# One instruction order in place of another: the Tile scheduler of a two-layer trunk set to its timeline simulation

## Chip, cores and metric

The kernel runs on one core of a Trainium2 chip. The metric is the device time of one execution in microseconds (us), as the median of several runs. An execution under the profiler gives the trace; its times are counted from the start of its span. TensorE (PE) is the matrix engine, PEld its weight loads, VectorE is DVE, ScalarE is ACT, GpSimd is POOL, SyncE is SP (SPq its DMA queue).

## What is computed

Two layers over 528 tokens (16 learned ones ahead of 512) of 1024 channels, in float32. Cut to what matters, each layer of the reference is:

```python
xn = _rmsnorm(h, pre_norm_g[l])
proj = xn @ w_in[l] + b_in[l]
c_h, c_b, c_c, c_z, r_q, r_k, r_v, r_z, g_a, g_b = jnp.split(proj, split_at, axis=-1)
y_a = _short_conv_branch(c_h, c_b, c_c, c_z, conv_w[l], conv_b[l], w_conv_out[l])
y_b = _retention_branch(r_q, r_k, r_v, r_z, ret_gn_g[l], w_ret_out[l])
y = jax.nn.sigmoid(g_a) * y_a + jax.nn.sigmoid(g_b) * y_b
y = y @ w_o[l]
h = h + _rmsnorm(y, post_norm_g[l])
```

The retention branch has four heads. Each takes scores of rotated queries and keys times a decay, multiplies them with the values, and normalizes the result per token and head: `(out - mu) * rsqrt(var + eps)`, times a weight and a silu gate.

## The kernel before

Channels lie on the 128 partitions, tokens along the free dimension, cut into two halves of 264. A float32 product is made of three matmul passes: every operand is split (`split`, L141) into a high half, a cast on ScalarE (L142), and a low half, the difference on VectorE (L143); TensorE then adds high x high, high x low and low x high in PSUM. Weights come from HBM through SyncE's queue into a ring of buffers `raw`; their halves are `whi` and `wlo` (`whd` and `wld` for a fourth combination). The activations' halves are `Xh` and `Xl`.

The large projections are made by `Group` (L284): a block scheme with seven products instead of eight, so weights are first added on VectorE (L307 `raw`, L314 `raw`, L315 `t`), and partial results in the PSUM banks `pa`, `pb`, `pc` are evicted by ScalarE (`put`, L325) and added on VectorE (L356). Matmuls of these groups are L279. `Std` (L660, matmuls L648 by `ktiles`) makes plain tiles, at the start, at the layer boundary and for the first heads of the second layer. `RetOut` makes the output projection of a head (matmuls L244).

A retention head ends in a norm that crosses four engines. `attend` (L481) leaves outputs in PSUM; ScalarE squares them (L492), VectorE scales them by the weight (L493) and adds the squares (L496). `rstd_token` then sums over the partitions with small matmuls against `ones_d` (L370), VectorE adds the epsilon (L374, `nv`), GpSimd takes the power -1/2 (L375, `ny`), and `spread` brings the result back to all partitions by matmuls with the identity (L384), copied by ScalarE (L387). `normed` multiplies with it (L514).

```python
pp = pslot()
for c in range(nch):
    nc.tensor.matmul(pp[0:sc, 0, c:c + 1], sums[:, t0 + c * sc:t0 + (c + 1) * sc], ones_d[:, 0:1],
                     start=True, stop=True)
...
with tc.high_priority():
    nc.vector.tensor_scalar(v, pp[0:sc, 0, 0:nch], scale, eps, op0=ALU.mult, op1=ALU.add)
nc.gpsimd.tensor_tensor(y, v, mhalf[0:sc, 0:nch], op=ALU.pow)
```

The same two functions serve the layer boundary. `wo_half` makes the output projection of one token half; `norms` (L742) normalizes it, adds the residual, sums squares (L641: `ysum` for the projection, `hsum` for the residual), and scales for the next layer:

```python
def scaled(k):
    nc.vector.scalar_tensor_tensor(YB[:, k, sl], hts[k][:, sl], gpre_sb[:, l + 1, k:k + 1], R[:, sl],
                                   op0=ALU.mult, op1=ALU.mult)
    split(*plain(half, k), YB[:, k, sl])
```

So for each of eight channel blocks one L761 is followed by a high half (ScalarE, L142) and a low half (VectorE, L143, `Xl` for the first token half, `r` or `Xl` for the second). `opening` then runs the first tiles of the second layer block by block (L648).

The order of each engine's instructions is not the order of the source. `tile.TileContext` (L1256) collects the program with its dependencies and runs a simulation of the engines: whenever an engine is free there, it takes, of the instructions that are ready at that simulated time, the one with the highest priority. Priority is program order, raised inside `tc.high_priority()`. The order found so is fixed in the program; on the chip every engine works through its own list in order, and waits on semaphores.

## Time and profile before

| what | value |
|---|---|
| median of 3 runs | 1605.07 us (1603.92 to 1609.26) |
| the profiled execution | 1600.25 us, span 1598.4 us, mean granted clock 0.995 |
| TensorE busy | 1553.9 us (97%), 11762 instructions |
| weight loads busy | 1494.1 us (93%) |
| VectorE busy | 1168.9 us (73%), 1702 instructions |
| ScalarE busy | 910.2 us (57%), 1763 instructions |
| GpSimd busy | 28.9 us (2%), 23 instructions |
| HBM | 168.21 MB read, 4.26 MB written, 108 GB/s over the span |

How to read it: the busy time of an engine counts the time in which one of its instructions ran. A matmul's time overlaps that of the next one, so what one costs is read from how many start in a stretch, not from its own length. The granted clock is a share of full speed. In a timeline the first number is the start, the second the length, and the brackets hold the idle time of the engine before the instruction with what ended it. A power on GpSimd is one instruction, L375.

### The profile page before, as it was taken

How to read it: one execution, taken by the hardware profiler on the slowest of the kernel's cores; microseconds unless marked ns; L12 is line 12 of the kernel's file. 1: busy time of each engine (PE TensorE's matmuls, PEld its weight loads, DVE VectorE, ACT ScalarE, POOL GpSimd, SP SyncE). 2: the span in 40 equal slices, each digit the busy share in tenths (PEclk: the TensorE clock that was granted, in tenths of full speed). 3: DMA queues.
4: the chain of work that ended last, by engine and by line, in shares of the span. 5: the costliest groups of instructions: out<-in, count | busy, mean ns of one | idle time of the engine just before them, and what ended most of it. 6: DMA issues, size and time to landing. Idle time of an engine off the chain costs nothing.

```text
span 1598.4 us, 29227 instructions
## 1 busy us (share of the span) xinstructions
PE 1553.9 (97%) x11762; PEld 1494.1 (93%) x11762; DVE 1168.9 (73%) x1702; ACT 910.2 (57%) x1763; POOL 28.9 (2%) x23
## 2 busy tenths in 40 slices
PE   9999999899999999999999999999999999999998
PEld 9989999898999999999999998998998999999986
DVE  6996966776776788866376889678777777997542
ACT  6675565464565466655345666655654655676531
POOL 0000000001000000000000000000000000000000
PEclk9999999999999999999999999999999999999999
DMA  7132332232222243335321223222322223334421
GB/s 263 67 113 73 106 107 89 83 108 97 89 103 87 91 141 128 133 123 180 119 101 53 100 94 113 103 103 95 111 93 80 101 98 119 132 126 145 142 98 53
DMA packets 86039, 174.37 MB, mean 109 GB/s; under 512 B 11280, under 2 KB 15888, under 8 KB 85904
## 3 DMA queue, kind: packets, MB, share of 16 engines
q1 hardware_dynamic: 85760, 172.50, 31.2%
q8 instruction: 92, 1.51, 0.4%
q14 instruction: 43, 0.35, 0.1%
q10 hardware_dynamic: 144, 0.01, 0.0%
HBM read 168.21 MB, written 4.26 MB: 108 GB/s over the span
## 4 chain that ended last, share of the span: by engine, by line
PE 79%; DVE 10%; ACT 5%; issue 3%; DMA 3%; POOL 1%; SPq 0%; DVEq 0%; POOLq 0%; ACTq 0%
PE pb L279 25%; PE pp L244 15%; PE pc L279 13%; PE pp L648 7%; PE pa L279 6%; PE pp L481 4%; PE pp L1122 3%; PE pb L648 3%; DVE wlo L143 2%; PE pp L422 2%; DMA raw<-in_w_in 2%; ACT whi L142 2%; DVE r L143 1%; PE pp L384 1%; PE pp L447 1%
## 5 line engine op out<-in xcount | busy, mean ns | idle before, releaser
L143 DVE TENSOR_TENSOR wlo<-raw,whi 128x1024 fp32r<-128x1024 f32 (+2 forms) x358 | 392.7, 1107 | 120.4 <-ACT whi L142 117.5
L142 ACT CAST whi<-raw 128x1024 fp32r<-128x1024 f32 (+2 forms) x358 | 339.4, 959 | 227.8 <-PE pp L244 63.7
L279 PE MATMUL pb<-Xh,whi 128*128 128x264 f32 (+2 forms) x1008 | 287.7, 285 | 2.2 <-ACT pa L335 1.2
L279 PE MATMUL pb<-Xl,whi 128*128 128x264 f32 (+2 forms) x1008 | 285.0, 283 | 0.0
L279 PE MATMUL pb<-Xh,wlo 128*128 128x264 f32 (+2 forms) x1008 | 284.7, 283 | 0.1
L244 PE MATMUL pp<-r,whi 128*128 128x264 f32 (+1 forms) x1152 | 251.2, 325 | 5.6 <-ACT r L142 4.8
L279 PE MATMUL pc<-Xh,whi 128*128 128x264 f32 (+2 forms) x672 | 194.4, 289 | 8.1 <-ACT f L325 7.8
L244 PEld LDWEIGHTS pp<-r,whi 128*128 128x128 f32 x1152 | 176.3, 188 | 23.7 <-ACT r L142 5.9
L279 PEld LDWEIGHTS pb<-Xh,whi 128*128 128x128 f32 x1008 | 189.6, 188 | 4.4 <-ACT pa L335 1.6
L279 PE MATMUL pc<-Xl,whi 128*128 128x264 f32 (+2 forms) x672 | 192.0, 286 | 0.0
L279 PE MATMUL pc<-Xh,wlo 128*128 128x264 f32 (+2 forms) x672 | 191.5, 285 | 0.0
L279 PEld LDWEIGHTS pb<-Xl,whi 128*128 128x128 f32 x1008 | 189.6, 188 | 0.6
L279 PEld LDWEIGHTS pb<-Xh,wlo 128*128 128x128 f32 x1008 | 189.3, 188 | 0.5 <-DVE wlo L143 0.3
L244 PE MATMUL pp<-r,wlo 128*128 128x264 f32 (+1 forms) x576 | 153.1, 321 | 1.4 <-DVE wlo L143 1.4
L307 DVE TENSOR_TENSOR raw<-raw 128x512 f32<-128x512 f32 x168 | 115.1, 686 | 41.4 <-DMA raw<-in_w_in 40.9
L279 PEld LDWEIGHTS pc<-Xh,whi 128*128 128x128 f32 x672 | 128.0, 190 | 12.3 <-ACT f L325 11.2
L279 PEld LDWEIGHTS pc<-Xl,whi 128*128 128x128 f32 x672 | 127.9, 190 | 0.4
L279 PEld LDWEIGHTS pc<-Xh,wlo 128*128 128x128 f32 x672 | 127.8, 190 | 0.3
L244 PEld LDWEIGHTS pp<-r,wlo 128*128 128x128 f32 x576 | 95.3, 188 | 9.8 <-DVE wlo L143 2.0
L279 PE MATMUL pb<-Xh,whd 128*128 128x264 f32 (+2 forms) x336 | 96.7, 288 | 1.1 <-ACT f L325 1.1
L279 PE MATMUL pa<-Xh,whi 128*128 128x264 f32 (+2 forms) x336 | 96.7, 288 | 0.0
L279 PE MATMUL pa<-Xl,whi 128*128 128x264 f32 (+2 forms) x336 | 95.7, 285 | 0.0
(219 smaller groups left out, 3300.3 us busy)
## 6 DMA issues: line engine op xcount, KB each, us to landing
raw<-in_w_in SPq DMA_DIRECT2D x426, 256.0 KB, 2.9
raw<-in_w_ro SPq DMA_DIRECT2D x32, 512.0 KB, 3.2
raw<-in_w_in SPq DMA_DIRECT2D x20, 512.0 KB, 4.8
raw<-in_w_co SPq DMA_DIRECT2D x16, 512.0 KB, 3.2
raw<-in_w_o SPq DMA_DIRECT2D x16, 512.0 KB, 3.9
Dsb<-in_decay SPq DMA_DIRECT2D x8, 520.0 KB, 3.9
h1d<-f SPq DMA_DIRECT2D x8, 264.0 KB, 4.5
f<-h1d SPq DMA_DIRECT2D x8, 264.0 KB, 4.3
```

The lines of the kernel that those rows point to most:

```text
L142: nc.scalar.copy(dst_hi, src)
L143: nc.vector.tensor_tensor(dst_lo, src, dst_hi.bitcast(F32), op=ALU.subtract)
L244: nc.tensor.matmul(banks[i][:, 0:cols.n], wt(k)[:, msl], xs(k)[:, sl], start=(k == 0 and a == 0), stop=(k == nk - 1 and a == 2),)
L279: nc.tensor.matmul(o[:, 0:n], wt[:, k, :], xs[:, blk, k, HALF - n:], start=(first and k == 0 and a == 0), stop=(k == 3 and a == 2), skip_g ...
L307: nc.vector.tensor_tensor(r[:, 512:], r[:, 512:], r[:, 0:512], op=ALU.add)
L384: nc.tensor.matmul(pp[:, c // per, (c % per) * sc:(c % per + 1) * sc], y[:, c:c + 1].to_broadcast([sc, P]), ident[0:sc, 0:sc], start=True, ...
L422: nc.tensor.matmul(pp[0:kn, n + i, 0:cols.n], k[dt][x][:, k0:k0 + kn] if j < 4 else k8[:, dt * 2 + x, :], q[dt][y][:, sl], start=(dt == 0 ...
L447: nc.tensor.transpose(pp[0:kn, b, v * P:(v + 1) * P], vt[v][:, k0:k0 + kn] if j < 4 else v8[:, v, :], ident)
L481: nc.tensor.matmul(pp[:, b, lo_ - banks[b][0]:hi_ - banks[b][0]], V[j][x][0:kn, v * P:(v + 1) * P], S[0:kn, SOFF[j] + lo_ - q0:SOFF[j] + h ...
L648: nc.tensor.matmul(o, wt(k), xs[:, i0:], start=(k == 0 and a == 0), stop=(k == KD - 1 and a == 2))
L1122: nc.tensor.matmul(o, x[:, xs], wo[k][half][w], start=(k == 0 and a == 0), stop=(k == KD - 1 and a == 2))
```

## The change

The `TileContext` gets one more argument. The simulation that orders the instructions is then the framework's timeline simulation and no longer its core simulation. Instructions, tiles and dependencies are the same; only the order on each engine differs, and with it which buffer a tile gets and which wait stands where.

```diff
-    with tile.TileContext(nc) as tc:
+    with tile.TileContext(nc, schedule_with_timeline_sim=True) as tc:
         trunk(tc, *args)
```

GpSimd's order is the same in both. On SyncE some loads change places, mostly the decay tables and the inputs at the boundary. Three places of the other engines follow; names are the program's, with the number of the tile behind the underscore.

**First place: TensorE at the norm of the first head.** The groups beside it are those of the convolution, `pb_1726`, `pa_108` and `pc_1727`. Before:

```order
L279 MATMUL pb_1726<-Xh,whi_1565 128x264
L279 MATMUL pb_1726<-Xl,whi_1565 128x264
L279 MATMUL pb_1726<-Xh,wlo_1566 128x264
L370 MATMUL pp_1821<-ones_d,f_1522 88x1 x6
L279 MATMUL pa_108<-Xh,whi_1565 128x264
L279 MATMUL pa_108<-Xl,whi_1565 128x264
L279 MATMUL pa_108<-Xh,wlo_1566 128x264
```

After the change:

```order
L279 MATMUL pc_1727<-Xl,whi_1652 128x264
L279 MATMUL pc_1727<-Xh,wlo_1653 128x264
L279 MATMUL pb_1726<-Xh,whi_1652 128x264
L279 MATMUL pb_1726<-Xl,whi_1652 128x264
L370 MATMUL pp_1821<-ones_d,f_1522 88x1 x6
L279 MATMUL pb_1726<-Xh,wlo_1653 128x264
```

L370 has moved behind the 12 matmuls of `pa_108`, the 12 of `pc_1727` and 2 of the second round of `pb_1726`; L384 stood 36 rows behind L370 and stands 34 rows behind it now.

On VectorE at the same place, before:

```order
L307 TENSOR_TENSOR raw_1788<-raw_1788 128x512
L493 SCALAR_TENSOR_TENSOR f_1157<-pp_1740,gn_sb,f_1157 128x208
L493 SCALAR_TENSOR_TENSOR f_1157<-pp_1740,gn_sb,f_1157 128x320
L496 TENSOR_TENSOR f_1522<-f_1522,f_1761 128x528
L143 TENSOR_TENSOR wlo_1785<-raw_1393,whi_1784 128x1024
L143 TENSOR_TENSOR wld_1854<-t_1781,whd_1853 128x512
L570 TENSOR_TENSOR f_1335<-f_1495,f_1335 128x528
L374 TENSOR_SCALAR nv_1828<-pp_1821 88x6
L315 TENSOR_TENSOR t_1940<-raw_1572 128x512
L143 TENSOR_TENSOR wlo_1847<-raw_1455,whi_1846 128x1024
L143 TENSOR_TENSOR wlo_1895<-raw_1569,whi_1894 128x1024
```

After the change:

```order
L493 SCALAR_TENSOR_TENSOR f_1157<-pp_1740,gn_sb,f_1157 128x208
L307 TENSOR_TENSOR raw_1788<-raw_1788 128x512
L143 TENSOR_TENSOR wlo_1785<-raw_1393,whi_1784 128x1024
L493 SCALAR_TENSOR_TENSOR f_1157<-pp_1740,gn_sb,f_1157 128x320
L496 TENSOR_TENSOR f_1522<-f_1522,f_1761 128x528
L143 TENSOR_TENSOR wld_1854<-t_1781,whd_1853 128x512
L570 TENSOR_TENSOR f_1335<-f_1495,f_1335 128x528
L315 TENSOR_TENSOR t_1940<-raw_1572 128x512
L143 TENSOR_TENSOR wlo_1847<-raw_1455,whi_1846 128x1024
L374 TENSOR_SCALAR nv_1828<-pp_1821 88x6
L314 TENSOR_TENSOR raw_1791<-raw_1788,raw_1850 128x512
L143 TENSOR_TENSOR wlo_1895<-raw_1569,whi_1894 128x1024
```

The first L493 now runs ahead of L307 and a low half (`wlo_1785`) ahead of the second; L374 has moved behind `wlo_1847`, and L314 stands behind it, which needs the load of `raw_1850`.

**Second place: the layer boundary, first token half.** TensorE before, where L370 with `pp_9710` stands 35 rows ahead of this piece, among the matmuls of `pp_9697`:

```order
L648 MATMUL pp_9697<-Xl,r_9181 128x264
L648 MATMUL pp_9697<-Xh,r_9182 128x264
L384 MATMUL pp_9754<-ident,ny_9715 128x88 x3
L648 MATMUL pb_9820<-Xh,whi_9187 128x264
L648 MATMUL pb_9821<-Xh,whi_9193 128x264
L648 MATMUL pp_9822<-Xh,whi_9203 128x264
L370 MATMUL pp_9847<-ones_d,ysum 88x1 x3
L648 MATMUL pb_9820<-Xl,whi_9187 128x264
```

After the change:

```order
L648 MATMUL pp_9697<-Xl,r_9181 128x264
L648 MATMUL pp_9697<-Xh,r_9182 128x264
L370 MATMUL pp_9710<-ones_d,hsum 88x1 x3
L384 MATMUL pp_9754<-ident,ny_9715 128x88 x3
L648 MATMUL pb_9820<-Xh,whi_9187 128x264
L648 MATMUL pb_9821<-Xh,whi_9193 128x264
L648 MATMUL pp_9822<-Xh,whi_9203 128x264
L648 MATMUL pb_9820<-Xl,whi_9187 128x264
```

L370 with `pp_9710` has moved to the end of that tile, with L384 right behind it; the L370 of the other sum (`pp_9847`) has moved to a later place.

VectorE at the boundary, before:

```order
L374 TENSOR_SCALAR nv_9714<-pp_9710 88x3
L143 TENSOR_TENSOR Xl<-raw_9175,Xh 128x512
L143 TENSOR_TENSOR Xl<-raw_9185,Xh 128x512
L143 TENSOR_TENSOR Xl<-raw_9199,Xh 128x512
L143 TENSOR_TENSOR Xl<-raw_9201,Xh 128x512
L761 SCALAR_TENSOR_TENSOR YB<-f_9219,gpre_sb,f_9254 128x264
L641 TENSOR_TENSOR ysum<-ysum,f_9784 128x264
L761 SCALAR_TENSOR_TENSOR YB<-f_9220,gpre_sb,f_9254 128x264
L641 TENSOR_TENSOR ysum<-ysum,f_9788 128x264
L143 TENSOR_TENSOR Xl<-YB,Xh 128x264
L374 TENSOR_SCALAR nv_9851<-pp_9847 88x3
```

After the change:

```order
L143 TENSOR_TENSOR Xl<-raw_9201,Xh 128x512
L374 TENSOR_SCALAR nv_9714<-pp_9710 88x3
L761 SCALAR_TENSOR_TENSOR YB<-f_9219,gpre_sb,f_9254 128x264
L761 SCALAR_TENSOR_TENSOR YB<-f_9220,gpre_sb,f_9254 128x264
L761 SCALAR_TENSOR_TENSOR YB<-f_9221,gpre_sb,f_9254 128x264
L761 SCALAR_TENSOR_TENSOR YB<-f_9222,gpre_sb,f_9254 128x264
L761 SCALAR_TENSOR_TENSOR YB<-f_9223,gpre_sb,f_9254 128x264
L641 TENSOR_TENSOR ysum<-ysum,f_9784 128x264
L761 SCALAR_TENSOR_TENSOR YB<-f_9224,gpre_sb,f_9254 128x264
L761 SCALAR_TENSOR_TENSOR YB<-f_9225,gpre_sb,f_9254 128x264
L761 SCALAR_TENSOR_TENSOR YB<-f_9226,gpre_sb,f_9254 128x264
L143 TENSOR_TENSOR Xl<-YB,Xh 128x264
```

L374 has moved behind the four `Xl` of `raw`, and all eight L761 stand ahead of the first `Xl` of `YB`, where two stood.

**Third place: VectorE at the boundary, second token half.** Before:

```order
L374 TENSOR_SCALAR nv_10039<-pp_10035 88x3
L761 SCALAR_TENSOR_TENSOR YB<-f_9219,gpre_sb,f_9254 128x264
L761 SCALAR_TENSOR_TENSOR YB<-f_9220,gpre_sb,f_9254 128x264
L761 SCALAR_TENSOR_TENSOR YB<-f_9221,gpre_sb,f_9254 128x264
L143 TENSOR_TENSOR r_9793<-YB,r_9791 128x264 x2
L143 TENSOR_TENSOR r_9794<-YB,r_9792 128x264
L761 SCALAR_TENSOR_TENSOR YB<-f_9222,gpre_sb,f_9254 128x264
```

After the change:

```order
L761 SCALAR_TENSOR_TENSOR YB<-f_9219,gpre_sb,f_9254 128x264
L761 SCALAR_TENSOR_TENSOR YB<-f_9220,gpre_sb,f_9254 128x264
L761 SCALAR_TENSOR_TENSOR YB<-f_9221,gpre_sb,f_9254 128x264
L761 SCALAR_TENSOR_TENSOR YB<-f_9222,gpre_sb,f_9254 128x264
L761 SCALAR_TENSOR_TENSOR YB<-f_9223,gpre_sb,f_9254 128x264
L761 SCALAR_TENSOR_TENSOR YB<-f_9224,gpre_sb,f_9254 128x264
L761 SCALAR_TENSOR_TENSOR YB<-f_9225,gpre_sb,f_9254 128x264
L761 SCALAR_TENSOR_TENSOR YB<-f_9226,gpre_sb,f_9254 128x264
L143 TENSOR_TENSOR r_9793<-YB,r_9791 128x264 x2
```

All eight L761 stand ahead of the first low half `r_9793`, where three stood.

## Rows read from the trace of the kernel before

**Rows 1.** Page, part 1: busy time, share of the span, instructions.

```profile
PE 1553.9 (97%) x11762; PEld 1494.1 (93%) x11762; DVE 1168.9 (73%) x1702; ACT 910.2 (57%) x1763; POOL 28.9 (2%) x23
```

**Rows 2.** Windows: busy us of each engine (instructions), granted TensorE clock, DMA share, GB/s.

```profile
141.00:148.00 7.00, 6.66 (x34) 6.69 (x35) 4.24 (x7) 2.72 (x6) 1.71 (x1) 0.52 0.11 37
151.00:179.00 28.00, 27.31 (x222) 26.89 (x221) 27.76 (x39) 19.45 (x38) 0.00 (x0) 1.00 0.36 124
550.00:600.00 50.00, 50.00 (x414) 50.00 (x413) 40.83 (x56) 31.07 (x53) 0.00 (x0) 1.00 0.36 127
```

**Rows 3.** Waits of TensorE: us in total, times, longest us.

```profile
PE pc L279 <- ACT f L325: 7.8, 9, 1.6
PE pp L384 <- POOL ny L375: 6.5, 4, 3.0
...
PE pp L370 <- DVE f L496: 4.2, 3, 3.3
PE pb L648 <- ACT Xh L142: 1.7, 1, 1.7
```

**Rows 4.** Timeline of TensorE, 141 to 149: start, length, [idle before, what ended it].

```profile
141.34 1.89 PE L370 MATMUL pp<-ones_d,f 128*88 128x1 f32 x12 [3.33 <-DVE f L496]
...
148.24 0.28 PE L279 MATMUL pc<-Xh,wlo 128*128 128x264 f32 x1
```

**Rows 5.** Timeline of TensorE at the layer boundary.

```profile
814.91 0.80 PE L384 MATMUL pp<-ident,ny 88*128 88x88 f32 x6
...
817.89 0.56 PE L370 MATMUL pp<-ones_d,ysum 128*88 128x1 f32 x6
818.31 0.37 PE L648 MATMUL pb<-Xl,whi 128*128 128x264 f32 x1
```

**Rows 6.** Timeline of VectorE and the DMA queue (SPq), 138 to 152.

```profile
138.49 0.69 DVE L307 TENSOR_TENSOR raw<-raw 128x512 f32<-128x512 f32 x1 [1.60 <-DMA raw<-in_w_in]
...
140.50 0.70 DVE L496 TENSOR_TENSOR f<-f,f 128x528 f32<-128x528 f32 x1
...
146.98 1.22 DVE L143 TENSOR_TENSOR wlo<-raw,whi 128x1024 fp32r<-128x1024 f32 x1 [2.76 <-ACT whi L142]
150.96 1.22 DVE L143 TENSOR_TENSOR wlo<-raw,whi 128x1024 fp32r<-128x1024 f32 x1 [2.75 <-ACT whi L142]
...
148.23 0.33 SPq L301 DMA_DIRECT2D raw<-in_w_in  x1
```

**Rows 7.** Page, part 6: DMA issues, KB each, median us to landing.

```profile
raw<-in_w_in SPq DMA_DIRECT2D x426, 256.0 KB, 2.9
```

**Rows 8.** Timelines of VectorE at 282 and of GpSimd, head two and head four.

```profile
282.57 0.71 DVE L143 TENSOR_TENSOR r<-f,r 128x528 fp32r<-128x528 f32 x1 [0.70 <-ACT r L142]
...
278.34 4.71 POOL L375 TENSOR_TENSOR ny<-nv,mhalf 88x6 f32<-88x6 f32 x1 [132.93 <-DVE nv L374]
...
504.63 1.32 POOL L375 TENSOR_TENSOR ny<-nv,mhalf 88x6 f32<-88x6 f32 x1 [108.03 <-DVE nv L374]
```

**Rows 9.** Timelines of VectorE and of GpSimd at the layer boundary.

```profile
810.83 0.16 DVE L374 TENSOR_SCALAR nv<-pp 88x3 f32<-88x3 f32 x1 [0.33 <-PE pp L370]
813.11 2.50 DVE L143 TENSOR_TENSOR Xl<-raw,Xh 128x512 fp32r<-128x512 f32 x4 [2.12 <-ACT Xh L142]
816.16 0.49 DVE L761 SCALAR_TENSOR_TENSOR YB<-f,gpre_sb,f 128x264 f32<-128x264 f32 x1 [0.55 <-ACT f L387]
...
817.66 0.42 DVE L143 TENSOR_TENSOR Xl<-YB,Xh 128x264 fp32r<-128x264 f32 x1
...
811.07 0.84 POOL L375 TENSOR_TENSOR ny<-nv,mhalf 88x3 f32<-88x3 f32 x1 [16.73 <-DVE nv L374]
```

**Rows 10.** Timelines of VectorE and of TensorE, 844 to 846.

```profile
844.11 1.30 DVE L761 SCALAR_TENSOR_TENSOR YB<-f,gpre_sb,f 128x264 f32<-128x264 f32 x3 [5.29 <-ACT f L387]
845.33 1.11 DVE L143 TENSOR_TENSOR r<-YB,r 128x264 fp32r<-128x264 f32 x3
...
845.81 0.39 PE L648 MATMUL pp<-r,whi 128*128 128x264 f32 x1 [0.32 <-DVE r L143]
```

## The prediction

> **What bounds the kernel now.** I read the page first, for the busiest engine [rows 1]: TensorE is busy 1553.9 of 1598.4 us, so its idle time is 44.5 us. A busy TensorE need not be one at its peak, so the windows come next [rows 2]: in a stretch without a wait, 50.00 us hold 414 matmuls, 0.121 us for one of 128x264, at a granted clock of 1.00; behind one wait the clock stands at 0.52. The order of instructions cannot shorten a matmul; it can only move waits, and what the clock loses behind them. The waits of TensorE by what ended them [rows 3] name three families: an eviction by ScalarE (L325) that frees a PSUM tile, 7.8 us over nine places; the spreading matmul (L384) that wants the power of GpSimd (L375), 6.5; the summing matmul (L370) that wants the squares of VectorE (L496), 4.2, of which 3.3 in one place. What there is to win is thus some 3% in all, spread over many places, and a new order can make as many waits as it takes away. I therefore compared the two orders at each place where TensorE waits, and at those to which a wait could move; four carry over 1 us.
>
> The sum is made against the profiled execution, 1600.25 us, which stands 4.8 us (0.3%) under the median of the runs, 1605.07. I add the difference that I find to the median. About 0.3% (4.8 us) is also what a measurement of this kernel can tell from no change.
>
> **Part A: the first retention head's norm, near 141 us.** In the old order TensorE stands 3.33 us at L370, and then runs at half the clock [rows 4], granted 0.52 [rows 2]. From the start of L370 to the matmul at 148.24 lie 6.90 us, which hold L370's 12 small matmuls and 23 pitches. Six such small ones took 0.42 us elsewhere (817.89 to 818.31 [rows 5]), so 12 are 0.84; 23 x 0.121 is 2.8. The fall thus costs 6.90 - 0.84 - 2.8 = 3.2 us. L370 was late because of VectorE [rows 6]: L307 waited 1.60 us for its weights, two L493 and L496 stood behind it, and L496 ended at 141.2. The new order puts the first L493 ahead of L307, which wins nothing for L496: L307 still ends at 139.2, a low half (1.2 us) now follows, then L493 and L496, so L496 ends near 141.3 again. What changes is on TensorE's side: 26 matmuls that do not need the sums now stand ahead of L370. 26 x 0.121 = 3.1 us, so of the wait 0.2 stay. With a wait that short I expect no fall of the clock: 3.1 + 3.2 = 6.3 us won.
>
> What is late next is VectorE. From 151 to 179 us it is busy 27.76 of 28 us [rows 2], so TensorE keeps its gain only as far as that stretch begins earlier too. In the old order it began at 150.96, when a high half arrived from ScalarE [rows 6]. In the new order L314, then the low half, then L307 stand at its head, and L314 needs a load that is issued only when the low half ahead of it has freed a buffer (148.23, behind the low half of 146.98 [rows 6]). That low half now stands ahead of L374 and should run from 143.2 to 144.4, since its high half waits for a matmul group that runs some 3.5 us earlier. The load then takes 2.9 us [rows 7]: the stretch starts at about 147.3, 3.7 earlier than before. The gain lies between 3.7 (VectorE sets everything) and 6.3 (TensorE had slack there). I take 5.0, the middle, since neither end is nearer.
>
> One thing could take it back, the power on GpSimd. At 278 us, where more work of VectorE followed L374 at once, the power lasted 4.71 us, until 1.2 us after VectorE's first pause (282.57 - 0.70 = 281.87); with VectorE idle behind L374 it took 1.32 [rows 8]. In the new order L314 stands behind L374; it waits for its load, VectorE pauses, and the power ends in that pause, before L384 is due (34 matmuls, 4.1 us, behind L370). So the power costs nothing in the sum. The Trainium skill (SBUF — State Buffer, section "SBUF: two separate sides") calls the ports that VectorE and GpSimd share an exclusive lock, which the instruction that starts first holds for that one instruction; by that rule the power would wait for one VectorE instruction at most and the gain of part A would be safe with or without the pause. The 4.71 us are more than such a turn (a low half, the longest instruction here, takes 1.22 [rows 6]), so the measurement decides, and a rival keeps a chance for it.
>
> **Part B: heads two and three, near 283 and 397 us.** Here 24 matmuls move from between L370 and L384 to ahead of L370, so L384 stands bare behind L370. But L384 was bound by the power, not by L370 [rows 3, 8]: VectorE does the same work by the same time, L374 moves to near its end, and the power still ends about 1.2 us behind the pause. TensorE has done the same matmuls by then. Difference 0 at both, from -0.3 to +0.5.
>
> **Part C: the layer boundary, 810 to 822 us.** In the old order L370 stood in the middle of its last tile, 35 matmuls (4.2 us) ahead of L384, and L384 started without a wait at 814.91 [rows 5]. In the new one they all stand ahead of L370, and L384 straight behind it. On VectorE L374 moves behind the four Xl, which end at 815.6 [rows 9], where it ran at 810.83. From L374 to the end of the power it takes 0.24 + 0.84 us (810.83 to 811.07, and the power with VectorE idle [rows 9]): L384 at 816.7, 1.8 us later. The first L761 came 1.25 us behind L384 (816.16), now at 817.95. Then the order on VectorE decides: before, the first low half Xl followed 1.50 us after the first L761 (817.66). Now all eight L761 and an L641 stand ahead of it, nine instructions at 0.407 (three in 1.22 us [rows 10]): 3.7 us. Xl starts at 821.6 and ends at 822.0. TensorE has three matmuls that need high halves only; L370, which stood behind them, now comes later (0.42 us). Its first Xl matmul moves from 818.31 to 822.0. Loss: 3.7 + 0.4 = 4.1 us, with nothing beside it, since TensorE's order has nothing else there. Bounds: 2.0, if ScalarE's casts and the four Xl with them come sooner; 7.3, if the idle pieces drop the clock once (3.2, part A).
>
> **Part D: the second half of the boundary, 843 to 848 us.** The same on the other half: eight L761 ahead of the first low half r, where three stood. TensorE took that r at 845.81 [rows 10]. Now 844.11 + 8 x 0.407 = 847.4, plus 0.4 for r: 847.8. Loss 2.0; bounds 0.4 (if matmuls that the new order puts between cover most) and 5.2 (with a fall).
>
> **Elsewhere.** Evictions and splits move by a few places at a dozen points. A wait of that sort cost 7.8 / 9 = 0.9 us on the mean and 1.6 at most [rows 3]. I count four that go (near 112, 521, 742 and 1304 us) and four that come (near 62, 900, 975 and 1033 us): 0, from -3 to +4. SyncE's order changes only among loads that are needed much later, GpSimd's not at all.
>
> **Sum.** -5.0 + 0 + 4.1 + 2.0 + 0 = +1.1 us: 1601.4 by the profiled execution, **1606 us** by the median.
>
> **The rivals.**
> *The gain stands and the boundary is covered.* If VectorE's and ScalarE's work at the boundary runs while TensorE still ends the tile before, C and D cost their lower bounds, 2.0 and 0.4, and A gives 6.3; with 2 us of the small waits that is -6: 1599. For it: VectorE was idle from 811.0 to the Xl at 813.11 [rows 9]. Against: the eight L761 all need the copy behind L384.
> *The boundary drops the clock.* The place is 815 to 822 us: TensorE has some 5 us idle there in three pieces, and 3 more near 845. The clock fell behind the wait of 3.33, not behind the 1.7 for Xh [rows 3, 4]; the longest piece now is about 2.5. If a piece like it is enough, 3.2 come on in C and, for a shorter one, half of that in D: 1.1 + 4.8 = +5.9, 1611. It decides from somewhere between 1.7 and 3.3 us idle at a stretch.
> *The power is caught in part A.* If that load has landed before L374, VectorE does not pause, the power lasts 4.71 us or more, L384 waits, the clock falls again, and A gives nothing: +6.1, 1611.
> *Nothing comes of it*, since VectorE's full stretches pace both orders: A, C and D shrink together, within the forecast's own range.
>
> **How the numbers follow.** The forecast (-4.8 to +4.8 around the median) gets 0.47, the first rival 0.24, the clock 0.20, the power 0.06, other losses 0.03. Faster by over 0.3% is the first rival, slower the last three: 0.24, 0.47, 0.29. The range goes from 2 us below the first rival to 4 above the second and third (small waits at their upper bound): 1597 to 1615.
>
> **What would show it right or wrong.** Right: no wait of 3 us near 141 and a granted clock of 1.00 there; the two waits of 3 us at L384 still there, on GpSimd; new waits at L384 and at the first Xl matmul between 812 and 823, some 4 us more than before, and 2 more at the first r. Wrong: a wait at the first head's L384, VectorE's full stretch ending as late as before, a fall of the clock near 820, or waits on L325 and L244 that differ by over 4 us in sum.

## The result and the profile after

| | before | after |
|---|---|---|
| median of 6 runs each | 1604.79 us | 1621.63 us |
| lowest and highest | 1603.92 to 1609.26 | 1618.82 to 1627.65 |
| the profiled execution, span | 1600.25 us, 1598.4 | 1620.42 us, 1618.6 |
| mean granted clock of it | 0.995 | 0.985 |

The change makes the kernel **slower**: the ratio of the times is 1.0106, with a 95% interval of 1.0084 to 1.0128, some 17 us. The forecast was 1606 us, the range ended at 1615. One run of the window from 862 to 1060 us, further down, took 6061.18 us; its median and ratio there are those of the other five.

The page after, part 1, beside [rows 1]:

```profile
PE 1558.1 (96%) x11762; PEld 1504.6 (93%) x11762; DVE 1171.2 (72%) x1702; ACT 912.6 (56%) x1763; POOL 18.6 (1%) x23
```

The counts are the same. TensorE's idle time is 1618.6 - 1558.1 = 60.5 us, where it was 44.5: of the 20.2 us between the two spans 16.0 are idle time, and 4.2 are a longer busy time of the same instructions, at a mean granted clock of 0.985 in place of 0.995. The waits of TensorE after, in the order of the view (with [rows 3] for before):

```profile
PE pc L279 <- ACT f L325: 8.4, 7, 1.8
PE pp L648 <- ACT f L981: 7.8, 2, 6.7
PE pp L384 <- POOL ny L375: 7.0, 5, 2.5
...
PE pp L422 <- ACT f L988: 2.3, 1, 2.3
...
PE pb L648 <- DVE Xl L143: 1.8, 1, 1.8
PE pb L648 <- ACT Xh L142: 1.7, 1, 1.7
...
PE pp L648 <- ACT f L790: 1.6, 1, 1.6
```

The wait for L496 (4.2 in three, the longest 3.3 [rows 3]) is gone, as part A had it. The largest single wait, 6.7 us of L648 for an eviction L981, has no part of its own in the prediction, nor has the one of L422: "Elsewhere" counts a wait that comes near 62 us and one near 900, at 0.9 us each.

Where the time went shows best when every TensorE instruction is matched with itself in the other trace. I took its start after minus its start before, and the median of these over the 20 us of the old trace that begin at the time given (a number worked out from the two timelines; "late" means that the new order is behind):

| old time, us | late, us | what lies between this row and the one above it |
|---|---|---|
| 120 | 11.9 | the first tiles and the first rotations |
| 140 | 5.3 | the first head's norm (part A) |
| 260 | 6.8 | VectorE's full stretch behind it |
| 280 | 5.5 | head two (part B) |
| 800 | 1.9 | heads three and four, the output projections |
| 880 | 9.4 | the layer boundary (parts C and D) |
| 1060 | 19.8 | the second layer's first head |
| 1580 | 20.3 | the rest |

So two places that the prediction put under "Elsewhere" at nothing cost 12 and 10 us in this pair of traces: the entry, up to 115 us, and the second layer's first head, from 862.

**The entry.** VectorE after, the timeline from 36 to 58:

```profile
45.59 5.53 DVE L997 SCALAR_TENSOR_TENSOR YB<-YB,gpre_sb,f 128x528 f32<-128x528 f32 x8 [0.29 <-ACT f L387]
51.03 3.18 DVE L984 TENSOR_TENSOR f<-f,f 128x528 f32<-128x528 f32 x5
...
54.72 0.70 DVE L708 TENSOR_TENSOR f<-YB 128x528 f32<-128x528 f32 x1
```

and the same engine before:

```profile
39.10 3.48 DVE L997 SCALAR_TENSOR_TENSOR YB<-YB,gpre_sb,f 128x528 f32<-128x528 f32 x5
42.50 0.70 DVE L708 TENSOR_TENSOR f<-YB 128x528 f32<-128x528 f32 x1
```

The first norm's L384 stands further back on TensorE (43.28 us, where it ran at 36.96), so its copy L387 comes later, and VectorE's chain starts at 45.59 in place of 39.10. From there to about 80 us VectorE is full in both traces, so the delay stays; and its list is another one, in which additions L984 stand ahead of the block sums L708. What comes late at the end are the rotations. The last of their four products L405 came at 73.41 before, and comes at 88.15 now; the second came at 64.85, and comes at 80.87 now. Before and after:

```profile
64.85 0.69 DVE L405 TENSOR_TENSOR f<-f,f 128x528 f32<-128x528 f32 x1
```

```profile
80.87 0.71 DVE L405 TENSOR_TENSOR f<-f,f 128x528 f32<-128x528 f32 x1
```

Of these 16.0 us only 6.5 are the later start of the chain; the rest comes of what now stands ahead of the rotation in VectorE's list. On ScalarE the evictions of the plain tiles stand, as before, behind the cast and the copies of this second rotation:

```profile
81.61 0.63 ACT L142 CAST r<-f 128x528 fp32r<-128x528 f32 x1 [3.42 <-DVE f L405]
82.15 0.69 ACT L392 CAST r<-r 128x128 fp32r<-128x128 f32 x3
82.75 0.65 ACT L981 COPY f<-pp 128x264 f32<-128x264 f32 x2
```

and TensorE stands until the tile is free; after it the windows show the clock at half:

```profile
83.45 0.59 PE L648 MATMUL pp<-Xh,whi 128*128 128x264 f32 x1 [6.70 <-ACT f L981]
```

```profile
70.00:80.00 10.00, 6.75 (x48) 6.54 (x47) 10.00 (x17) 3.36 (x5) 0.00 (x0) 0.84 0.19 63
80.00:90.00 10.00, 6.55 (x33) 6.55 (x34) 7.86 (x13) 4.35 (x13) 0.00 (x0) 0.54 0.04 15
```

33 matmuls started from 80 to 90 us, where 67 did before, at a clock of 1.00.

**The second layer's first head.** VectorE, ScalarE and TensorE after:

```profile
908.03 0.69 DVE L405 TENSOR_TENSOR f<-f,f 128x512 f32<-128x512 f32 x1
```

```profile
908.94 1.04 ACT L142 CAST whi<-raw 128x1024 fp32r<-128x1024 f32 x1 [3.17 <-issue]
909.89 0.61 ACT L142 CAST r<-f 128x512 fp32r<-128x512 f32 x1
910.41 0.83 ACT L988 ACTIVATE f<-pp,bin 128x256 f32<-128x256 f32 x2
```

```profile
908.58 0.28 PE L279 MATMUL pa<-Xl,whi 128*128 128x258 f32 x1
...
911.30 2.49 PE L422 MATMUL pp<-r,r 128*80 128x512 f32 x6 [2.32 <-ACT f L988]
```

L314 has moved ahead of the second rotation on VectorE and waits there 1.73 us for weights. The rotation's L405 ran at 895.26 before and runs at 908.03 now, 3.4 us later than the 9.4 us by which TensorE is late at 880. But L405 is not what TensorE waited for last. It has ended at 908.72, and its cast on ScalarE (909.89) still stands behind a cast of weights. That one starts at 908.94, just behind the end of TensorE's last matmul but one with `pa` (908.58 + 0.28 = 908.86). In the old list the cast of the rotation and the evictions L988 stand ahead of that cast of weights:

```profile
896.34 0.61 ACT L142 CAST r<-f 128x512 fp32r<-128x512 f32 x1
896.85 0.84 ACT L988 ACTIVATE f<-pp,bin 128x256 f32<-128x256 f32 x2
...
899.67 1.05 ACT L142 CAST whi<-raw 128x1024 fp32r<-128x1024 f32 x1
```

So by this trace ScalarE's own order makes up to 1.2 us of the 2.32 (909.89 - 908.72), and an earlier L405 alone would have changed nothing.

### The profile page after: what moved, and what is told of

It reads as the page before. It is cut to its first block, busy times and chain, and to the rows that moved or that the text cites. A ratio compares the mean times of both kernels' runs of the same rounds, so it can differ in the third digit from the quotient of the medians.

```text
span 1618.6 us, 29287 instructions
## 1 busy us (share of the span) xinstructions
PE 1558.1 (96%) x11762; PEld 1504.6 (93%) x11762; DVE 1171.2 (72%) x1702; ACT 912.6 (56%) x1763; POOL 18.6 (1%) x23
## 4 chain that ended last, share of the span: by engine, by line
PE 85%; DVE 8%; ACT 3%; DMA 2%; issue 2%; POOL 0%; SPq 0%; DVEq 0%; POOLq 0%; ACTq 0%
PE pb L279 27%; PE pc L279 15%; PE pp L244 14%; PE pp L648 7%; PE pa L279 7%; PE pp L481 5%; PE pb L648 3%; PE pp L1122 3%; DVE wlo L143 2%; DMA raw<-in_w_in 2%; PE pp L422 2%; ACT whi L142 1%; PE pp L384 1%; PE pp L447 1%; DVE r L460 0%
## 5 line engine op out<-in xcount | busy, mean ns | idle before, releaser
L244 PE MATMUL pp<-r,whi 128*128 128x264 f32 (+1 forms) x1152 | 248.2, 322 | 5.7 <-ACT r L142 4.9
L244 PEld LDWEIGHTS pp<-r,whi 128*128 128x128 f32 x1152 | 177.0, 188 | 21.4 <-ACT r L142 6.2
L244 PE MATMUL pp<-r,wlo 128*128 128x264 f32 (+1 forms) x576 | 153.0, 321 | 3.1 <-DVE wlo L143 3.1
L307 DVE TENSOR_TENSOR raw<-raw 128x512 f32<-128x512 f32 x168 | 115.8, 689 | 54.3 <-DMA raw<-in_w_in 53.1
L279 PEld LDWEIGHTS pc<-Xh,whi 128*128 128x128 f32 x672 | 128.7, 192 | 12.7 <-ACT f L325 10.5
L244 PEld LDWEIGHTS pp<-r,wlo 128*128 128x128 f32 x576 | 95.4, 188 | 11.3 <-DVE wlo L143 3.7
L279 PE MATMUL pb<-Xl,whd 128*128 128x264 f32 (+2 forms) x336 | 96.0, 286 | 0.0
L279 PE MATMUL pb<-Xh,wld 128*128 128x264 f32 (+2 forms) x336 | 95.9, 285 | 0.0
```

Source lines behind the costliest of these rows:

```text
L244: nc.tensor.matmul(banks[i][:, 0:cols.n], wt(k)[:, msl], xs(k)[:, sl], start=(k == 0 and a == 0), stop=(k == nk - 1 and a == 2),)
L279: nc.tensor.matmul(o[:, 0:n], wt[:, k, :], xs[:, blk, k, HALF - n:], start=(first and k == 0 and a == 0), stop=(k == 3 and a == 2), skip_g ...
L307: nc.vector.tensor_tensor(r[:, 512:], r[:, 512:], r[:, 0:512], op=ALU.add)
```

## The experiments

In all of them the source is that of the kernel before. The order is no longer left to the scheduler: a table names each engine's instructions one after another, and each is made to depend on the one ahead of it, without a semaphore. With it any stretch can have the new order and the rest the old one; what differs between the kernels is the table alone. The old order fixed by a table in the same way was not timed by itself; b_785 below, which moves 22 instructions of VectorE, takes 1.0011 of the time before, so fixing the order costs little.

```diff
+def _fix_order(tc, nc):
+    dep = mybir.DependencyInfo(mybir.DependencyClass.NoSync, mybir.DependencyReason.DATA)
...
+        for a, b in zip(names, names[1:]):
+            tc.add_manual_dep(seen[b], a, dep, reason="order")
...
     with tile.TileContext(nc) as tc:
         trunk(tc, *args)
+        _fix_order(tc, nc)
```

A window is given in us of the old trace: those instructions of an engine that started in it stand in the new order among themselves. The median of the kernel before lay between 1605.88 and 1606.84 us in the four sets of runs beside which these were timed.

### The six windows

```diff
-    every engine: the old list
+    every engine: the new list for what ran from 0 to 115 us, the old one else      (w_entry)
+    ... from 115 to 200 us       (w_head0)
+    ... from 200 to 785 us       (w_mid)
+    ... from 785 to 862 us       (w_bound)
+    ... from 862 to 1060 us      (w_l2head0)
+    ... from 1060 us to the end  (w_rest)
```

The entry:

> The old order everywhere, the new one only for the instructions that the old trace starts in the first 115 us. Theory A (each place keeps what it loses): TensorE is 11.8 us late at 115 us in the new trace, so this kernel is 12 us slower (9 to 14), with the wait of about 6.9 us for an eviction of L981 near 83 us. Theory B (the delay is only lent, the waits near 141 us and the full stretch of VectorE take it back): 3 to 6 us slower, and no wait of 3 us at the first L370.

The first head's norm:

> The old order everywhere, the new one only from 115 to 200 us (the norm of the first retention head). Theory A: 4 to 7 us faster, the wait of 3.3 us at L370 and the fall of the clock behind it are gone, as in part A of the prediction. Theory B: the wait vanished in the new trace only because TensorE came late there, so alone this window gives 0 to -2 us, and a wait of over 2 us stays near 141 us.

Heads two to four:

> The old order everywhere, the new one only from 200 to 785 us (the other heads and groups of the first layer). Theory A (the places add up, as the trace shows them): in the new trace the lateness goes from 7.4 us at 200 to 1.9 at 780, so this window alone is 4 to 6 us faster. Rival (the medians must add up: 17 in all less the four windows measured): 10 to 14 us faster.

The layer boundary:

> The old order everywhere, the new one only from 785 to 862 us (the layer boundary). Theory A: 8 to 9 us slower as in the new trace (1.2 late before, 9.9 behind), with two falls of the clock, near 820 and 850 us. Rival (the order alone costs the waits, the falls come from the state that the new order before it left): 5 to 6 us slower and no fall.

The second layer's first head:

> The old order everywhere, the new one only from 862 to 1060 us (the first head of the second layer). Theory A: 10 us slower (8 to 11), with waits near 900 (L422), 920 and 965 (L325) and 975 us (L244) and falls of the clock behind one or two of them. Rival (these waits are followers of the boundary's delay): under 3 us slower, none of those waits over 1.5 us.

The rest:

> The old order everywhere, the new one only from 1060 us to the end. Theory A: lateness 19.8 at 1060 and 20.3 at the end of the new trace, so no difference beyond 2 us. Rival (the medians must add up): 2 to 5 us faster.

| window | median, us | ratio, 95% interval | as us |
|---|---|---|---|
| w_entry | 1619.30 | 1.0083 [1.0070, 1.0096] | +13.3 |
| w_head0 | 1602.47 | 0.9977 [0.9966, 0.9989] | -3.7 |
| w_mid | 1601.00 | 0.9963 [0.9948, 0.9977] | -5.9 |
| w_bound | 1616.41 | 1.0061 [1.0046, 1.0075] | +9.8 |
| w_l2head0 | 1615.97 | 1.0073 [1.0052, 1.0094] | +11.7 |
| w_rest | 1603.33 | 0.9975 [0.9962, 0.9987] | -4.0 |

The last column is the ratio less one, times the median before. The sum is +21; the whole change has +17. Each interval reaches 1.8 to 3.4 us to either side, so the six add up within what they are known to. Theory A came true at the entry, in heads two to four and in the second layer's first head, and at the boundary nearly so (9.8 for 8 to 9). w_head0 lies between the two theories (3.7 for 4 to 7 or 0 to 2), with the trace that theory A described. In w_rest theory A failed: the traces before and after showed no difference there (19.8 and 20.3 late), the runs gain 4.0, as the rival had it; where they gain it was not looked for.

The large waits come back where the new order has them. Outside the windows the traces are not alike, though all lists are the old ones there. That of w_head0 loses 4.4 us from 260 to 800 and 3.7 from 1060 on, with falls of the clock that are longer than those in the trace before, or that it has not. So a window is judged by the medians. In w_entry TensorE stands before the same matmul as in the kernel after, and from 115 to 260 us it is 11 to 12 us late:

```profile
83.08 0.59 PE L648 MATMUL pp<-Xh,whi 128*128 128x264 f32 x1 [8.23 <-ACT f L981]
```

In w_head0, less the 1.9 us that it was late ahead of the window, it is 6.9 us early at 160 and 4.1 at 200: won at the norm, and partly given back in VectorE's stretch. In w_l2head0 it loses 10.3 us from 862 to 1060.

### The two that gain, together

```diff
-    every engine: the old list
+    every engine: the new list from 115 to 785 us and from 1060 us on, the old one else
```

> The new order on all engines from 115 to 785 us and from 1060 us to the end of the old trace, the old order in the rest (the first rope, the layer boundary, the first head of the second layer). If what the windows do adds up, the sum is -3.7 (115 to 200) -6.0 (200 to 785) -4.0 (from 1060) = about -13 us: 1591 to 1596, ratio 0.990 to 0.994, with the wait before head 1's norm and its clock fall gone. If the gains share a cause (runs of the new order merely drew fewer falls of the clock), or are given back at the seams, -3 to -7 us: 1599 to 1603, ratio 0.9955 to 0.998.

1596.80 us (1593.57 to 1597.26), ratio 0.9932 [0.9918, 0.9947]: 10.9 us faster than before and 25 faster than after, the fastest order of all. It lies 2 to 3 us short of the sum of its windows; the ratio is inside the range of the first theory. In its trace the stretch where L370 used to wait has no wait and the full clock:

```profile
140.00:147.00 7.00, 7.00 (x65) 7.00 (x63) 4.04 (x6) 3.90 (x7) 1.33 (x1) 1.00 0.23 77
```

### The entry: which engine, and which move

```diff
-    every engine: the new list from 0 to 115 us                      (w_entry)
+    TensorE alone the new list from 0 to 115 us                      (e_pe)
+    VectorE and ScalarE alone the new list from 0 to 115 us          (e_dveact)
+    w_entry, with VectorE's L708 to L711 of the first block ahead of the five L984   (e_sums)
+    the old list, with L384, L387 and four L997 of the first norm further ahead      (e_early)
```

> As the first window (0 to 115 us), but with the new order on TensorE alone; VectorE, ScalarE and the loads keep the old one. There L384 of the first norm stands 21 rows later. Theory C (the late L384 starts VectorE's full stretch later, and that is paid one for one): 21 x 0.121 = 2.5 us for the rows and what TensorE is late by then, so 3 to 6 us slower, VectorE full from about 41 instead of 38 us. Theory D (VectorE's and ScalarE's own order inside the stretch starves TensorE, L384 only shifts work that has slack): under 1.5 us slower, no wait of over 2 us between 60 and 90 us.

> As the first window, but with the new order on VectorE and ScalarE alone; TensorE keeps the old one, so L384 stands where it stood. Theory C: under 5 us slower, a wait of under 4 us for L981 near 80 us. Theory D: 9 us or more slower, with a wait of 6 us or more for L981 near 80 us, since the eviction still stands behind a cast that needs the last of the rotations on VectorE.

> The new order from 0 to 115 us on all engines, but on VectorE the first four sums of blocks (L708 to L711) stand ahead of the five additions L984 again, as in the old order. Theory that TensorE waits at the entry for these sums and their halves: they start 3 to 4 us earlier and the kernel takes 2 to 4 us less than with the whole window (1619.3), ratio 1.0055 to 1.007. Rival, that the last rotations at 80 to 88 us and the evictions behind them set the end of the entry: these end no earlier, the stall of 8 us near 83 stays, and so does the time, ratio 1.0075 to 1.009.

> The old order, with the first norm's six transposes (L384), its evictions (L387) and four of VectorE's additions behind them (L997) put ahead: the opposite of what the new order does with them. Theory C, that the time when VectorE's full stretch starts sets the end of the entry: it starts 2 to 4 us earlier and the kernel gains 2 to 5 us, ratio 0.997 to 0.9988. Rival D, that VectorE's start is not what counts (the new order's 12 us at the entry come from what stands on VectorE and ScalarE near 65 to 83 us): within 1.5 us, ratio 0.999 to 1.001.

| kernel | chain L997 starts | fourth L405 | late at 120, us | median, ratio |
|---|---|---|---|---|
| before | 39.10 | 73.41 | 0 | |
| e_early | 39.61 | 75.74 | 2.3 | 1608.56, 1.0010 [1.0000, 1.0021] |
| e_pe | 43.66 | 77.95 | 10.1 | 1615.00, 1.0049 [1.0031, 1.0068] |
| w_entry | 45.21 | 87.78 | 11.0 | 1619.30, 1.0083 [1.0070, 1.0096] |
| e_dveact | 43.69 | 88.08 | 21.8 | 1629.78, 1.0129 [1.0106, 1.0152] |

TensorE's order alone puts L384 back and costs 8 us, more than the 3 to 6 of theory C. VectorE's and ScalarE's order alone costs 21, as theory D had it (9 or more). The pair tells what makes the rotations late. VectorE's chain starts at the same time in both (43.66 and 43.69), but the fourth L405 comes at 77.95 in e_pe and at 88.08 in e_dveact: the late start passes through one for one, and VectorE's and ScalarE's lists add 10 us to it. The wait for L981 goes with these lists. It stands in e_dveact, where TensorE has its old order,

```profile
83.38 0.59 PE L648 MATMUL pp<-Xh,whi 128*128 128x264 f32 x1 [6.57 <-ACT f L981]
```

and not in e_pe, which loses its time elsewhere, at a high half of weights (and at an eviction L325 at 113.59, 3.19 us):

```profile
67.46 0.39 PE L279 MATMUL pc<-Xh,whi 128*128 128x264 f32 x1 [3.95 <-ACT whi L142]
```

e_dveact costs more than all together; a reading of this, not tried by itself, is that TensorE in the old order asks earlier for what VectorE now makes later.

e_sums holds one suspect against the other. The block sums start at 50.87 there in place of 54.35 in w_entry, but the fourth L405 comes no earlier (89.25), the wait stays,

```profile
84.55 0.59 PE L648 MATMUL pp<-Xh,whi 128*128 128x264 f32 x1 [8.45 <-ACT f L981]
```

and so does the time: 1618.86 us, ratio 1.0081 [1.0064, 1.0098]. With the whole window, what holds the entry up is not the block sums but the rotations and the evictions that stand behind them on ScalarE.

e_early missed its aim. L384 ran 2.7 us earlier (34.22), but ScalarE's copy L387 had to stay behind an eviction that waits for a matmul further on, so L387 came at 38.97, later than before (38.46). VectorE's block sums slipped by 2.3 us and so did TensorE's work from 60 us on. The expected gain of an earlier start is thus not tried, and the runs (1.0010, an interval that touches no change) tell no loss from noise.

### The boundary: VectorE, and its three pieces

```diff
-    every engine: the new list from 785 to 862 us       (w_bound)
+    VectorE alone the new list from 785 to 862 us       (b_dve)
+    VectorE alone, 785 to 810.5 us: ahead of L374       (b_785)
+    VectorE alone, 810.5 to 826 us: part C              (b_810_5)
+    VectorE alone, 826 to 862 us: part D                (b_826)
```

> The new order from 785 to 862 us on VectorE alone, the old one on all other engines and in the rest. Theory that VectorE's order makes the boundary's loss: the stall at the boundary behind VectorE's block sums and the one near 854 stay, with falls of the clock near 820 and 855: +8 to +10 us, ratio 1.005 to 1.0065, as when all engines take the new order there. Rival, that it needs TensorE's own moves at the boundary: within 4 us of the kernel before, ratio under 1.0025, and at most one of the two falls.

> VectorE alone in the new order from 785 to 810.5 us, that is ahead of the norm's L374 (the residual's additions L757, the sums of squares L641 and the first four low halves Xl of raw in another order); all else as before. Theory that a place which the prediction did not see makes a part of the loss: L384 near 815 comes 2 us or more later, +2 to +6 us, ratio 1.0012 to 1.004. Rival, that the loss lies in the two places that it saw: within 1 us, ratio 0.999 to 1.001.

> VectorE alone in the new order from 810.5 to 826 us (L374 behind the four low halves of raw, eight L761 ahead of the first low half of YB), all else as before: part C of the prediction by itself. By its sum +4.1 us, ratio 1.0025; with one fall of the clock +7.3, ratio 1.0045; the first low half of YB 4 us later than in the kernel before. If the loss of VectorE's order lies elsewhere: within 1.5 us, ratio under 1.001.

> VectorE alone in the new order from 826 to 862 us (eight L761 ahead of the first low half r of the second token half, and the rope's first product ahead of four splits), all else as before: part D by itself. By the prediction's sum +2.0 us, ratio 1.0012; with a fall of the clock near 850 +3.6 to +5.2, ratio 1.002 to 1.0032. If it is covered: within 0.6 us.

| kernel | median, us | ratio, 95% interval | as us |
|---|---|---|---|
| b_dve | 1619.83 | 1.0079 [1.0063, 1.0096] | +12.7 |
| b_785 | 1606.73 | 1.0011 [0.9998, 1.0024] | +1.8 |
| b_810_5 | 1613.21 | 1.0043 [1.0028, 1.0058] | +6.9 |
| b_826 | 1610.87 | 1.0016 [1.0002, 1.0030] | +2.6 |

VectorE's order is enough for the whole loss (12.7 us, where all engines together lose 9.8; the two intervals overlap), and the rival is refuted; the pieces add up to 11.3. The piece ahead of L374, which the prediction did not price, is small, and its interval touches no change. The runs of b_826 spread from 1604.50 to 1613.27, so its size is known to 2 us at best. In b_810_5 VectorE shows what part C described:

```profile
819.01 2.11 DVE L761 SCALAR_TENSOR_TENSOR YB<-f,gpre_sb,f 128x264 f32<-128x264 f32 x5 [2.40 <-ACT f L387]
...
822.60 0.43 DVE L143 TENSOR_TENSOR Xl<-YB,Xh 128x264 fp32r<-128x264 f32 x1
```

The first low half comes 4.9 us later than in [rows 9]; the kernel was 0.9 us late before the window began, so 4.0 us are its own, where part C had 3.9 (821.6 for 817.66). TensorE stood 1.61 us for the power, 1.71 for Xh as before [rows 3], and 4.15 at L370. In TensorE's old list this L370 stands ahead of the first matmul with Xl, and it wants the sum `ysum` that VectorE's new list puts off; so the kernel tries VectorE's side of part C and not TensorE's. The clock fell:

```profile
825.06 1.04 PE L370 MATMUL pp<-ones_d,ysum 128*88 128x1 f32 x6 [4.15 <-DVE ysum L641]
```

```profile
820.00:832.00 12.00, 7.58 (x39) 7.37 (x40) 6.44 (x18) 2.79 (x8) 0.85 (x1) 0.57 0.15 57
```

The trace lost 9.1 us here, the runs 6.9. In b_826 the eight L761 take 3.24 us to the first r, TensorE stands 2.34 us there, where it stood 0.32 [rows 10], and the trace lost 3.3.

### The second layer's first head, first wait alone

```diff
-    every engine: the new list from 862 to 1060 us      (w_l2head0)
+    every engine: the new list from 862 to 922 us       (l2a)
```

> The new order from 862 to 922 us on all engines, the old one in the rest. Theory that the loss of this head sits in its first wait (the second rotation behind the decay weights on VectorE, then the casts behind it on ScalarE, near 911 us of the changed kernel's trace: 2.48 us and a fall of the clock): +5 to +7 us, ratio 1.003 to 1.0045, with the wait before L422 and a fall within 2 us of it. Rival, that the later waits of the same head (935, 981, 994, 1051 us) carry the loss: within 3 us, ratio under 1.002.

1613.74 us, ratio 1.0046 [1.0030, 1.0061], some 7.4 us [4.8, 9.8] of the 11.7, a little above the 5 to 7 of the theory; the rival is refuted. The same wait stands in its trace, and the clock falls behind it:

```profile
911.80 1.80 PE L422 MATMUL pp<-r,r 128*80 128x512 f32 x6 [2.32 <-ACT f L988]
```

```profile
911.00:918.00 7.00, 6.20 (x32) 5.56 (x33) 3.96 (x6) 4.80 (x16) 0.00 (x0) 0.76 0.22 75
```

As in the kernel after, the cast of weights on ScalarE starts (909.45) when the second rotation's L405 has already ended (909.10). The remaining 4 us, with the waits at 935 to 1051 us of the trace after, were not taken apart further. Nor was that cast, or L314, moved by itself: which of them makes the wait is read from the trace, not shown by a run.

## Why the prediction was wrong, point by point

**What bounds the kernel: right.** TensorE's instructions are the same, its waits and its clock are what moved. **Wrong was the step that bounded the waits to come:** "I count four that go (near 112, 521, 742 and 1304 us) and four that come (near 62, 900, 975 and 1033 us): 0, from -3 to +4." Priced by the mean of the L325 waits (0.9 us), the places were taken as single waits of one eviction. The runs give +13.3 for the entry, -5.9 for 200 to 785 us, +11.7 for the second layer's first head, -4.0 for the rest: +15.1 in place of 0, with both the losses and the gains larger than the bounds. What was left out is what stands ahead of the awaited instruction on its own engine. At the entry the second rotation comes 16.0 us later on VectorE, 6.5 by the late start behind L384 and the rest by VectorE's own list; its cast and then the evictions stand behind it on ScalarE, and TensorE gets this back as 6.70 us. Near 900 a cast of weights on ScalarE has moved ahead of the rotation's cast and the evictions. The lists of both engines had moved at these places; I did not follow the wait from one engine to the next there, as I did in parts A and C. What saves the 5.9 and the 4.0 us stays open.

**Part A: right for TensorE; for VectorE the size came out by luck.** L370 and L384 now run without a wait, and the clock is full:

```profile
152.00:159.00 7.00, 7.00 (x65) 7.00 (x64) 3.93 (x7) 3.90 (x7) 1.33 (x1) 1.00 0.23 77
```

The power fell into VectorE's pause, as worked out: VectorE stands 2.42 us for L314's weights, and the power takes 1.33:

```profile
153.95 0.16 DVE L374 TENSOR_SCALAR nv<-pp 88x6 f32<-88x6 f32 x1 [0.38 <-PE pp L370]
156.53 0.69 DVE L314 TENSOR_TENSOR raw<-raw,raw 128x512 f32<-128x512 f32 x1 [2.42 <-DMA raw<-in_w_in]
```

```profile
154.19 1.33 POOL L375 TENSOR_TENSOR ny<-nv,mhalf 88x6 f32<-88x6 f32 x1 [117.37 <-DVE nv L374]
```

TensorE won 6.6 us at the norm (6.3 was worked out) and kept 4.1 at 200 us in w_head0, 3.7 by the runs: the lower bound, 3.7, rather than the middle, 5.0. But the bound was not reached in the way it was worked out. L496 does not end "near 141.3 again": it ends at 140.30 in w_head0, which less the 1.9 us that this kernel is late by then is 138.4, since L307 and its weights come 3.2 us sooner (137.19 - 1.9 for 138.49). The low half and the load behind it come sooner too, and L314 opens VectorE's stretch at 146.57 - 1.9 = 144.7, in place of 147.3, 6.3 us ahead of the old start. The load did take 2.9 us (from 143.63). TensorE gave 2.5 us back only later, of it 1.4 at L244, which waits 1.85 us for a low half where it waited 0.47:

```profile
146.57 0.69 DVE L314 TENSOR_TENSOR raw<-raw,raw 128x512 f32<-128x512 f32 x1 [2.41 <-DMA raw<-in_w_in]
```

```profile
171.54 0.52 PE L244 MATMUL pp<-r,wlo 128*128 128x264 f32 x2 [1.85 <-DVE wlo L143]
```

**Part B: right in mechanism, a little short in size.** L384 still waits for the power in head two, 2.37 us, where it was 3.01:

```profile
288.62 1.57 PE L384 MATMUL pp<-ident,ny 88*128 88x88 f32 x12 [2.37 <-POOL ny L375]
```

The power lasts 1.72 us there, where it lasted 4.71 [rows 8], since L374 has moved nearer to VectorE's first pause. GpSimd's and VectorE's rows:

```profile
286.84 1.72 POOL L375 TENSOR_TENSOR ny<-nv,mhalf 88x6 f32<-88x6 f32 x1 [131.32 <-DVE nv L374]
```

```profile
288.07 0.71 DVE L143 TENSOR_TENSOR r<-f,r 128x528 fp32r<-128x528 f32 x1 [0.70 <-ACT r L142]
```

It ends at 288.56, 1.2 us behind the pause (288.07 - 0.70 = 287.37), the same distance as before. The pause itself is 5.5 us late (287.37 for 281.87) where TensorE was 6.8 late, so the head won 1.3 us in this trace, where 0.3 was the most that was forecast.

**Parts C and D: right in place, C in mechanism too; too small in size.** L384 at 817.92, less the 1.9 us that the kernel was late by then, is 816.0 (forecast 816.7); the first matmul with Xl is at 823.34 - 1.9 = 821.4 (forecast 822.0):

```profile
817.92 0.90 PE L384 MATMUL pp<-ident,ny 88*128 88x88 f32 x6 [1.25 <-POOL ny L375]
820.54 0.81 PE L648 MATMUL pb<-Xh,whi 128*128 128x264 f32 x2 [1.72 <-ACT Xh L142]
823.34 0.59 PE L648 MATMUL pb<-Xl,whi 128*128 128x264 f32 x1 [1.77 <-DVE Xl L143]
```

At the second half the wait that ends last is not part D's: TensorE's new list wants an eviction L790 there (the low half r runs at 853.96, 0.3 us behind it). With VectorE's order alone, in b_826, it is part D's own wait, 2.34 us for r.

```profile
853.67 0.58 PE L648 MATMUL pp<-r,whi 128*128 128x264 f32 x1 [1.58 <-ACT f L790]
```

And the clock fell behind the pieces, here and at the second half:

```profile
819.00:827.00 8.00, 4.69 (x22) 4.39 (x22) 7.36 (x19) 4.04 (x12) 0.00 (x0) 0.57 0.37 134
853.00:858.00 5.00, 4.33 (x21) 4.17 (x22) 3.79 (x11) 2.58 (x8) 0.00 (x0) 0.66 0.00 0
```

The runs give +9.8 where C and D had 4.1 + 2.0 = 6.1. The difference, 3.7, is near the 4.8 that the rival "the boundary drops the clock" put on top; this rival came true in its places, with C's upper bound of 7.3 beside 6.9 measured and D's 0.4 to 5.2 around 2.6 (both with VectorE's order alone). How much of the 3.7 is the clock's stays open: of the twelve kept traces in which all engines have the old order there, eight show a fall near 820 us of the old time too, so a part of its cost is in the median before already. The 0.20 that this rival got rested on one sentence, that the clock fell behind 3.33 us and not behind 1.7, and this was one execution.

**The sum by what was measured:** -3.7 (A and what follows to 200) + 9.8 (C, D) + 15.1 (elsewhere) = +21, against +17 [13.5, 20.5] for the whole change.

## What to carry to other kernels

When a scheduler rewrites whole lists, look for each instruction that the bounding engine awaits at what has moved ahead of it on its own engine, and follow the delay from queue to queue until it is back at the bounding engine; a count of single waits misses the places where two engines hand it on. An order need not be taken whole: here the new order is better in two stretches and the old one in the rest, and the joined one is 0.7% faster than before, where the change alone made it 1.06% slower. At the entry the order of VectorE and ScalarE, taken over without TensorE's, cost more than all together (1.0129 for 1.0083).

## What the runs showed of the hardware that I had not expected

The clock falls in some executions of a stretch and not in others, at a wait that is the same. The old order has a wait for Xh at the boundary [rows 3]. It is 1.71 us long in all twelve kept traces with the old order there (once 1.72), and the clock falls near it in eight of them and not in four. Three of them: it is 1.71 us in the timelines of the kernel before, of e_early and of l2a alike (at 817.42, 820.31 and 824.17). The windows behind it follow, first of the kernel before, at full clock:

```profile
820.00:828.00 8.00, 8.00 (x69) 8.00 (x68) 5.58 (x13) 2.32 (x6) 0.00 (x0) 1.00 0.10 40
```

then of e_early:

```profile
820.00:828.00 8.00, 7.69 (x39) 7.69 (x40) 6.56 (x18) 3.11 (x8) 0.97 (x1) 0.57 0.49 163
```

and of l2a:

```profile
824.00:832.00 8.00, 7.83 (x41) 7.83 (x42) 6.42 (x18) 2.98 (x8) 0.97 (x1) 0.57 0.40 146
```

The runs of the old order agree with this: they go from 1600.25 us at a mean clock of 0.995 to 1612.58 at 0.990. The profiled execution of the kernel before was the quickest of all its runs, so the limit between 1.7 and 3.3 us that the prediction read from it does not hold, and a loss found between two profiles (9.1 us in b_810_5, say) may differ by 2 or 3 us from that between the medians (6.9). What decides whether the clock falls at such a wait stays open.
